# Latent scalings and rotary key-row copies: from VectorE to ScalarE in a two-layer hybrid block

## The chip, the core and the metric

The kernel runs on one core of a Trainium2 chip. A core has a matrix engine (TensorE, PE in the profile), VectorE (DVE), ScalarE (ACT), GpSimd (POOL) and SyncE (SP), whose queue here issues nearly all transfers. Each engine works through its own list of instructions in order; semaphores hold an instruction until what it needs is there. Data lies in SBUF (128 partitions) and in PSUM, where the matrix engine writes its sums. The metric is the time of one execution in microseconds. Before the change it is 857.3 us, the median of three runs (856.71 to 858.69).

## The reference, cut to what matters

Two layers, each with 512 tokens of width 1024. In each layer the normed input is projected; one part of the projection goes through an RWKV-7 recurrence, one through a gated linear recurrence, one through a latent attention with 8 heads; the three results, each gated, are projected back and added to the stream. The change lies in the latent attention:

```python
q = (rms_norm(q_lat, q_norm_g) @ w_uq).reshape(B, T, N_HEADS, QK_NOPE + QK_ROPE)
kv = (rms_norm(kv_lat, kv_norm_g) @ w_ukv).reshape(B, T, N_HEADS, QK_NOPE + V_DIM)
k_rope = apply_rope(k_rope, cos, sin)
s = jnp.einsum('bqhd,bkhd->bhqk', qn, k_nope) + jnp.einsum('bqhr,bkr->bhqk', qr, k_rope)
```

`q_lat` has 256 columns and `kv_lat` 128; each row of each is divided by its root mean square. `k_rope` has 32 columns, which all eight heads share.

## The kernel before

All tensors are fp32. A product of full precision is made of three matrix products (`mm3`, L232 to L235): each operand is split into a rounded part H, which ScalarE makes by a copy, and the rest L = x - H, which VectorE or GpSimd makes. `weights` (L217 to L230) does this for each piece of a weight matrix (tiles `wr`, `wH`, `wL`), `ysplit` (L387, through `split`, L209 to L211) for a result that goes into the output projection (tiles `c` in the profile). `copy` (L140) is a ScalarE activation that copies, with a factor if one is given.

A scheduler decides the order of the instructions on each engine from the order in the code and from its own estimates of durations, so moving an operation to another engine also shifts its neighbours. Buffers come from pools in which a new tile waits for the release of an old one: there are two rotating PSUM tiles `ps`, four PSUM accumulators `acc`, eleven SBUF tiles `g` (named `g2` in the code), three `hp` tiles.

The stage of the change comes once in each layer, in this order in the code:

- `latents(1)` (L918 to L937): for each of the four tiles `ln_t` of 128 tokens (448 columns: 256 of the query latent, 128 of the key and value latent, 32 + 32 of the rotated keys) ScalarE sums the squares (L922, L923), VectorE makes the reciprocal roots `rl` for all four tiles in one chain of small operations (L925, L926, `rsqrt` L198 to L203), and scales columns 0 to 255 (L930) and 256 to 383 (L931).
- `out_parts(1)` (L413 to L433): the output projection of the second branch, in two halves of 16 products of three; VectorE frees each accumulator at the end of a half (L428), and the second half takes the accumulators that the first leaves.
- `lat_step` (L954 to L967): PE transposes the four tiles of a column block into a `ps` tile (L962; L958 for the rotated keys), ScalarE makes H from it and VectorE L (L966).
- `ya_step` (L972 to L982): two transfers `bo` and `zz`, a product of both on GpSimd (L976), four transposes into a `ps` tile (L979), then on VectorE L980 (which also needs the GpSimd product), L981 and the split L211.
- `key_step` (L991 to L1005): for each of four pairs of heads three products and two copies of the result into `K2`; for the first pair the rotated key rows come from PSUM on ScalarE (L1001, L1002), for pairs 1 to 3 they are copied within `K2` from pair 0 (L1004, L1005), 64 partitions by 512 each.
- `value_step` and `query_step` (L1010 to L1029), then the scores, which read `K2`.

The string `Q1` (L65) mixes these steps: `a` is `ya_step`, `o` `out_parts`, `t` `lat_step`, `k`, `v` and `q` the key, value and query steps.

Of the kernel before, what the change touches and what calls it, by code (L numbers as in the profile page):

```python
# [12 lines left out]
ALU = mybir.AluOpType  # L13
# [34 lines left out]
def body(ctx, tc, x, wc, wl, wo, w2a2, gagx, wuq, wukv, vec, ln_g, fin_g, cst, out, depth=DEPTH):  # L48
    nc = tc.nc
    V, A, G = nc.vector, nc.scalar, nc.gpsimd  # L50
# [17 lines left out]
    def tl(tag, shape, dt=F32, bufs=1):  # L68
        cnt[0] += 1
        return SB.tile(list(shape), dt, tag=tag, name=f"{tag}_{cnt[0]}", bufs=bufs)  # L70

    def g2(shape=(128, 512)):
        return tl("g2", shape, F32, bufs=11)
# [10 lines left out]
    def am(shape):  # L84
        return tl("am", shape, F32, bufs=2)

    def sm(shape):
        return tl("sm", shape, F32, bufs=24)
# [21 lines left out]
    def acc(shape=(128, 512)):  # L110
        cnt[0] += 1
        return PS.tile(list(shape), F32, tag="acc", name=f"acc_{cnt[0]}", bufs=4)
# [27 lines left out]
    def copy(out, in_, **kw):  # L140
        i = A.activation(out=out, in_=in_, func=AF.Copy, **kw)  # L141
        return getattr(i, "ins", i)
# [52 lines left out]
    def rsqrt(ms, shape, tag=None):  # L195

        y, t = [tl(tag, shape, bufs=2) if tag else sm(shape) for _ in range(2)]
        V.tensor_scalar(out=y.bitcast(I32), in0=ms.bitcast(I32), scalar1=1, scalar2=None, op0=ALU.logical_shift_right)  # L198
        V.tensor_scalar(out=y.bitcast(I32), in0=y.bitcast(I32), scalar1=-1.0, scalar2=float(0x5F3759DF), op0=ALU.mult, op1=ALU.add)
        for _ in range(3):  # L200
            V.tensor_tensor(out=t, in0=y, in1=y, op=ALU.mult)
            V.scalar_tensor_tensor(out=t, in0=t, scalar=-0.5, in1=ms, op0=ALU.mult, op1=ALU.mult)
            V.scalar_tensor_tensor(out=y, in0=t, scalar=1.5, in1=y, op0=ALU.add, op1=ALU.mult)  # L203
        return y
# [12 lines left out]
    def weights(src, n=512, raw=None):  # L217

        if raw is None:
            raw = tl("wr", [128, n], F32, bufs=3)  # L220
            nc.sync.dma_start(out=raw, in_=src)
        H = tl("wH", [128, n], F32R, bufs=4)
        L = tl("wL", [128, n], F32R, bufs=4)
        wn[0] += 1
        i = copy(H, raw)
        if behind:
            tc.add_manual_dep(i, behind.pop(0).name, NOSYNC, reason="issue order")

        (V if wn[0] % wmod[0] == 0 or wn[0] <= 4 else G).tensor_tensor(out=L, in0=raw, in1=f(H), op=ALU.subtract)  # L229
        return H, L  # L230

    def mm3(o, a, b, start, stop):  # L232
        PE.matmul(o, a[0], b[0], start=start, stop=False)  # L233
        PE.matmul(o, a[0], b[1], start=False, stop=False)  # L234
        PE.matmul(o, a[1], b[0], start=False, stop=stop)  # L235
# [85 lines left out]
    def one_layer(l):  # L321
# [590 lines left out]
        def latents(part):  # L912
            if part == 0:
                for tt in range(4):
                    ln_t[tt] = g2([128, 448])
                    copy(ln_t[tt][:, 0:LAT], lat[tt])
                return
            kcos, ksin = misc["k"][:, 0], misc["k"][:, 1]  # L918
            lst = sm([128, 4, 2])
            for tt in range(4):  # L920
                j1, q = g2([128, 256]), ln_t[tt]
                A.activation(out=j1, in_=q[:, 0:256], func=AF.Square, scale=1.0 / 16.0, accum_out=lst[:, tt, 0:1])  # L922
                A.activation(out=j1[:, 0:128], in_=q[:, 256:384], func=AF.Square, scale=1.0 / 8.0, accum_out=lst[:, tt, 1:2])  # L923
            ms = sm([128, 4, 2])
            V.tensor_scalar(out=ms[:, :, 0:1], in0=lst[:, :, 0:1], scalar1=EPS, scalar2=None, op0=ALU.add)  # L925
            V.tensor_scalar(out=ms[:, :, 1:2], in0=lst[:, :, 1:2], scalar1=0.5, scalar2=EPS, op0=ALU.mult, op1=ALU.add)  # L926
            rl = rsqrt(ms, [128, 4, 2])
            for tt in range(4):
                q = ln_t[tt]
                V.tensor_scalar(out=q[:, 0:256], in0=q[:, 0:256], scalar1=rl[:, tt, 0:1], scalar2=None, op0=ALU.mult)  # L930
                V.tensor_scalar(out=q[:, 256:384], in0=q[:, 256:384], scalar1=rl[:, tt, 1:2], scalar2=None, op0=ALU.mult)  # L931
                a, b = tl("ro", [128, 32], bufs=4), tl("ro", [128, 32], bufs=4)
                V.tensor_tensor(out=a, in0=q[:, 384:416], in1=kcos[:, tt, :], op=ALU.mult)
                for d in range(2):
                    V.tensor_tensor(out=b[:, 16 * d:16 * d + 16], in0=q[:, 400 - 16 * d:416 - 16 * d], in1=ksin[:, tt, 16 * d:16 * d + 16], op=ALU.mult)
                for d in range(2):
                    V.tensor_tensor(out=q[:, 384 + 32 * d:416 + 32 * d], in0=a, in1=b, op=ALU.add)  # L937
# [4 lines left out]
        def b_split(_):  # L942
            yb[:] = [ysplit(y) for y in yb]

        steps.update({"H": chunk, "N": lambda _: group_norm(), "A": lru_a, "B": lambda i: lru_b(2 * i, 2 * i + 1), "R": b_sums, "Y": b_split,
                      "t": lat_products, "T": latents, "g": lambda p: gzc.append(gate(25 + p))})
        run(ORD2)
        run(ORD3)
# [40 lines left out]
        K2 = am([128, 4, 2, T])  # L989

        def key_step(p):  # L991
            if p == 0:
                WW["k"] = weights(wukv[l, :, 0:512])
            WK, kr = WW["k"], latT[3]
            o = acc()
            s = slice(p * 128, (p + 1) * 128)
            mm3(o, (WK[0][:, s], WK[1][:, s]), latT[2], True, True)
            copy(K2[0:64, p, 0, :], o[0:64, :])
            copy(K2[64:128, p, 1, :], o[64:128, :])
            if p == 0:  # L1000
                copy(K2[64:128, 0, 0, :], kr[0:64, :])  # L1001
                copy(K2[0:64, 0, 1, :], kr[0:64, :])  # L1002
            else:
                V.tensor_copy(out=K2[64:128, p, 0, :], in_=K2[64:128, 0, 0, :])  # L1004
                V.tensor_copy(out=K2[0:64, p, 1, :], in_=K2[0:64, 0, 1, :])  # L1005
        uvt = tl("UV", [128, 2, 2048])
        Vt = uvt[:, 0, :].rearrange("p (t h i) -> p t h i", t=4, h=8)
        PT = uvt[:, 1, :].rearrange("p (k t) -> p k t", k=4)
# [22 lines left out]
        for n, fn, c in (("k", key_step, 4), ("v", value_step, 4), ("q", query_step, 8)):  # L1031
            seqs[n] = [lambda fn=fn, i=i: fn(i) for i in range(c)]
# [193 lines left out]
```

## Time and profile before

| what | value |
| --- | --- |
| median of the runs | 857.3 us (856.71 to 858.69) |
| the profiled execution, its own time | 855.86 us |
| its span in the trace | 854.0 us |
| instructions in the trace | 15206 |
| mean granted clock of the matrix engine | 0.984 |
| stage of the change in layer 0, in layer 1 (us from the span's start) | about 298 to 325, 717 to 744 |

The profile's page gives busy times and groups of instructions by line. The trace gives more: the chain of waits (what ended last, followed back), the timeline of each engine with the idle time in front of an instruction and what ended it, and the busy time of each engine in stretches that one chooses. A group of helper lines (L141, L211, L229) is told apart by its tiles. Times in the timeline are starts and durations; a duration can overlap the next instruction's by some 0.06 us on VectorE and some 0.1 us on ScalarE, so the step from one start to the next is the better measure in a queue without gaps.

### The profile page before, as it was taken

What the parts mean: (1) busy time and instruction counts of PE and PEld (TensorE: products, weight loads), DVE (VectorE), ACT (ScalarE), POOL (GpSimd) and SP (SyncE); (2) the same over time, 40 slices, a digit from 0 to 9 for tenths busy, and PEclk for the clock granted to TensorE, in tenths of its full rate; (3) what the DMA queues carried; (4) which work ended last, traced back from release to release, by engine and by line L of the source; (5) the groups of instructions that cost most, each with busy time, mean ns of one, the idle gap of its engine ahead of it and who ended that gap; (6) DMA issues with size and microseconds to landing.
All of it is one profiled execution on the core that took longest, in us unless ns stands there. A gap on an engine that the chain in (4) does not pass through costs nothing.

```text
span 854.0 us, 15206 instructions
## 1 busy us (share of the span) xinstructions
PE 796.6 (93%) x5696; PEld 621.0 (73%) x5696; DVE 571.6 (67%) x1173; ACT 506.2 (59%) x990; POOL 325.7 (38%) x299
## 2 busy tenths in 40 slices
PE   4999999999879989999989999999998799999996
PEld 4878888877559867556778788888765697675674
DVE  5678777924886496774474966695367946877736
ACT  6667885656563536574467687846575435465644
POOL 0455557513352332012344556574143523310223
PEclk9999999999999999999999999999999899999999
DMA  7222224310123365123732233332101234731354
GB/s 245 96 74 84 72 93 136 117 51 27 32 77 97 124 197 184 51 87 99 268 124 90 75 99 101 98 111 94 29 25 41 81 107 129 241 114 50 111 173 162
DMA packets 49755, 91.08 MB, mean 107 GB/s; under 512 B 5520, under 2 KB 8336, under 8 KB 49680
## 3 DMA queue, kind: packets, MB, share of 16 engines
q1 hardware_dynamic: 49104, 89.05, 32.2%
q8 instruction: 45, 0.74, 0.4%
q10 hardware_dynamic: 576, 1.05, 0.3%
q14 instruction: 30, 0.25, 0.1%
HBM read 73.30 MB, written 16.78 MB: 105 GB/s over the span
## 4 chain that ended last, share of the span: by engine, by line
PE 69%; DVE 16%; ACT 8%; issue 3%; DMA 2%; POOL 1%; SPq 1%; ACTq 0%; DVEq 0%; POOLq 0%
PE acc L233 16%; PE acc L234 16%; PE acc L235 15%; PE acc L1058 4%; PE ck L1084 3%; ACT g L138 2%; PE ps L1076 2%; PE ps L687 1%; DVE g L681 1%; PE ps L611 1%; ACT UV L141 1%; ACT L136 1%; DVE wL L229 1%; PE ps L629 1%; PE ps L786 1%
## 5 line engine op out<-in xcount | busy, mean ns | idle before, releaser
L229 POOL TENSOR_TENSOR wL<-wr,wH 128x512 fp32r<-128x512 f32 (+1 forms) x126 | 169.7, 1350 | 290.0 <-ACT wH L141 266.0
L141 ACT ACTIVATE wH<-wr 128x512 fp32r<-128x512 f32 (+1 forms) x192 | 118.8, 622 | 140.6 <-PE acc L234 74.5
L233 PE MATMUL acc<-xH,wH 128*128 128x512 f32 (+1 forms) x496 | 192.7, 390 | 0.0
L234 PE MATMUL acc<-xL,wH 128*128 128x512 f32 (+1 forms) x496 | 189.7, 383 | 0.4 <-DVE xL L306 0.2
L235 PE MATMUL acc<-xH,wL 128*128 128x512 f32 (+1 forms) x496 | 189.1, 381 | 0.0
L233 PEld LDWEIGHTS acc<-xH,wH 128*128 128x128 f32 x496 | 94.3, 191 | 18.1 <-ACT xH L141 0.7
L235 PEld LDWEIGHTS acc<-xH,wL 128*128 128x128 f32 x496 | 94.3, 190 | 17.3
L234 PEld LDWEIGHTS acc<-xL,wH 128*128 128x128 f32 x496 | 94.4, 190 | 16.9 <-DVE xL L306 0.9
L229 DVE TENSOR_TENSOR wL<-wr,wH 128x512 fp32r<-128x512 f32 (+1 forms) x66 | 49.9, 760 | 72.8 <-ACT wH L141 72.7
L233 PE MATMUL acc<-wH,c 128*128 128x512 f32 x192 | 83.0, 432 | 2.6 <-DVE hp L428 1.3
L234 PE MATMUL acc<-wL,c 128*128 128x512 f32 x192 | 77.5, 404 | 0.5 <-DVE wL L229 0.5
L235 PE MATMUL acc<-wH,c 128*128 128x512 f32 x192 | 77.1, 402 | 0.0
L141 ACT ACTIVATE UV<-ps 64x512 f32<-64x512 f32 (+4 forms) x112 | 52.4, 494 | 30.9 <-PE ps L1076 22.6
L233 PEld LDWEIGHTS acc<-wH,c 128*128 128x128 f32 x192 | 36.7, 191 | 12.8 <-ACT c L141 3.0
L141 ACT ACTIVATE c<-g 128x512 fp32r<-128x512 f32 (+1 forms) x40 | 24.9, 630 | 34.3 <-DVE g L981 22.4
L138 ACT ACTIVATE c<-acc,sm 128x128 f32<-128x128 f32 (+3 forms) x64 | 33.6, 528 | 19.1 <-DVE sm L1060 18.8
L234 PEld LDWEIGHTS acc<-wL,c 128*128 128x128 f32 x192 | 36.9, 192 | 8.6 <-issue 1.4
L1058 PE MATMUL acc<-am,am 128*128 128x128 f32 (+3 forms) x128 | 42.3, 447 | 0.8 <-ACT c L138 0.8
L235 PEld LDWEIGHTS acc<-wH,c 128*128 128x128 f32 x192 | 36.8, 192 | 8.4 <-issue 0.5
L369 POOL TENSOR_TENSOR g<-g,g 128x512 f32<-128x512 f32 x24 | 32.1, 1338 | 24.1 <-ACT g L138 24.1
L136 ACT ACT_TABLE_LOAD x31 | 39.8, 1283 | 1.3 <-PEq L1214 0.7
L138 ACT ACTIVATE g<-g 128x512 f32<-128x512 f32 (+1 forms) x58 | 36.4, 627 | 4.6 <-DVE g L705 2.6
(222 smaller groups left out, 1592.4 us busy)
## 6 DMA issues: line engine op xcount, KB each, us to landing
wr<-in_wc_dram SPq DMA_DIRECT2D x116, 256.0 KB, 2.7
wr<-in_wo_dram SPq DMA_DIRECT2D x48, 256.0 KB, 3.4
hp<-dr SPq DMA_DIRECT2D x38, 256.0 KB, 3.2
dr<-hp SPq DMA_DIRECT2D x28, 256.0 KB, 2.1
dr<-g SPq DMA_DIRECT2D x16, 256.0 KB, 2.5
g<-dr SPq DMA_DIRECT2D x16, 256.0 KB, 3.6
wr<-in_wl_dram SPq DMA_DIRECT2D x16, 208.0 KB, 2.5
dr<-c SPq DMA_DIRECT2D x12, 256.0 KB, 3.4
```

The source lines that it names most:

```text
L136: chained(A.preload_act_table_set(SETS[st]))
L138: chained(A.activation(out=out, in_=in_, func=func, **kw))
L141: i = A.activation(out=out, in_=in_, func=AF.Copy, **kw)
L229: (V if wn[0] % wmod[0] == 0 or wn[0] <= 4 else G).tensor_tensor(out=L, in0=raw, in1=f(H), op=ALU.subtract)
L233: PE.matmul(o, a[0], b[0], start=start, stop=False)
L234: PE.matmul(o, a[0], b[1], start=False, stop=False)
L235: PE.matmul(o, a[1], b[0], start=False, stop=stop)
L369: G.tensor_tensor(out=z, in0=z, in1=s, op=ALU.mult)
L611: PE.matmul(os[e][:, cp, :].rearrange("p (x s) -> p x s", x=2), bk[rr, ch, :, :].rearrange("p x s -> p (x s)"), ar[rr, :, ch * 64:(ch + 1) ...
L1058: PE.matmul(o[:, 0:n], qT[:, hd, qt * 128:n], K2[:, p, e, 0:n], start=True, stop=True)
L1076: PE.transpose(o[:, (qt - kt) * 128:(qt - kt + 1) * 128], Pm[p][e, qt][:, kt * 128:(kt + 1) * 128], ident)
L1084: i = PE.matmul(ot[e * 64:(e + 1) * 64, k2 * 128:T], Vt[:, k2, 2 * p + e, :], PT[:, 2 * (k2 % 2) + e, 0:(4 - k2) * 128], start=(k2 == 0), ...
```

## The change

Eight scalings in each layer (L930, L931, four tiles) and six copies in each layer (L1004, L1005, three pairs) are issued on ScalarE, as activations that copy, the scalings with the column of `rl` as factor. Their operands, results and places in the code are the same.

```diff
@@ latents @@
-                V.tensor_scalar(out=q[:, 0:256], in0=q[:, 0:256], scalar1=rl[:, tt, 0:1], scalar2=None, op0=ALU.mult)
-                V.tensor_scalar(out=q[:, 256:384], in0=q[:, 256:384], scalar1=rl[:, tt, 1:2], scalar2=None, op0=ALU.mult)
+                copy(q[:, 0:256], q[:, 0:256], scale=rl[:, tt, 0:1])
+                copy(q[:, 256:384], q[:, 256:384], scale=rl[:, tt, 1:2])
@@ key_step @@
-                V.tensor_copy(out=K2[64:128, p, 0, :], in_=K2[64:128, 0, 0, :])
-                V.tensor_copy(out=K2[0:64, p, 1, :], in_=K2[0:64, 0, 1, :])
+                copy(K2[64:128, p, 0, :], K2[64:128, 0, 0, :])
+                copy(K2[0:64, p, 1, :], K2[0:64, 0, 1, :])
```

The scheduler's order shifts with it, in both layers alike. On ScalarE in layer 0 the scalings come behind the split of a weight (`wH_3342`); the last two of them and what follows read now (`g_509` is the fourth latent tile, `c_558` the first `ysplit`, `wH_3360` and `wH_3378` weights of the second half of `out_parts`, `c_584` to `c_588` the latents of `lat_step`):

```order
L141 ACTIVATE g_509_2938<-g_509_2938,sm_3071 128x256
L141 ACTIVATE g_509_2938<-g_509_2938,sm_3071 128x128
L141 ACTIVATE c_558_3137<-g_556_3126 128x512
L141 ACTIVATE wH_3360<-wr_3358 128x512
L141 ACTIVATE wH_3378<-wr_3376 128x512
L141 ACTIVATE c_584_3241<-ps_3236,vecs 128x512
L141 ACTIVATE c_586_3249<-ps_3244,vecs 128x512
```

`wH_3360` stood in front of `c_558` before and now stands behind it and behind all eight scalings.

On VectorE in layer 0, in the second half of the stage, from the third latent on (`c_588` the third latent, the tiles `g_591`, `g_595` and `g_599` are the `zz` of `ya_step` 1, 2 and 3, `am_3122` is `K2`), the order was before:

```order
L966 SCALAR_TENSOR_TENSOR c_588_3257<-ps_3252,vecs,c_588_3257 128x512
L1004 COPY am_3122<-am_3122 64x512 x3
L980 SCALAR_TENSOR_TENSOR g_591_3266<-ps_3270,vecs,g_591_3266 128x512
L1005 COPY am_3122<-am_3122 64x512
L981 TENSOR_TENSOR g_591_3266<-g_591_3266,g_590_3265 128x512
L980 SCALAR_TENSOR_TENSOR g_595_3281<-ps_3285,vecs,g_595_3281 128x512
```

and in the changed kernel:

```order
L966 SCALAR_TENSOR_TENSOR c_588_3257<-ps_3252,vecs,c_588_3257 128x512
L980 SCALAR_TENSOR_TENSOR g_591_3266<-ps_3270,vecs,g_591_3266 128x512
L981 TENSOR_TENSOR g_591_3266<-g_591_3266,g_590_3265 128x512
L980 SCALAR_TENSOR_TENSOR g_595_3281<-ps_3285,vecs,g_595_3281 128x512
L211 TENSOR_TENSOR c_593_3277<-g_591_3266,c_593_3277 128x512
L981 TENSOR_TENSOR g_595_3281<-g_595_3281,g_594_3280 128x512
```

The copies are gone from between L966 and the `ya_step` chain. On ScalarE, at the same place, they now stand in two groups of three ahead of the splits of that chain (`c_593`, `c_597`):

```order
L141 ACTIVATE am_3122<-ps_3260 64x512 x2
L141 ACTIVATE wH_3408<-wr_3406 128x512
L141 ACTIVATE am_3122<-am_3122 64x512 x3
L141 ACTIVATE c_593_3277<-g_591_3266 128x512
L141 ACTIVATE am_3122<-am_3122 64x512 x3
L141 ACTIVATE c_597_3292<-g_595_3281 128x512
```

On PE the transposes of the third latent block move from the last accumulator of a weight's round to the third, and three products of the key step move behind a value step. On SP a load (`bo` of `ya_step` 2) moves ahead of one store, and two weight loads of the query step move ahead of four stores of L430. GpSimd's order is the same.

## The prediction

> **What bounds the kernel now.** The page comes first: busy times, and the chain of work that ended last.
>
> ```profile
> PE 796.6 (93%) x5696; PEld 621.0 (73%) x5696; DVE 571.6 (67%) x1173; ACT 506.2 (59%) x990; POOL 325.7 (38%) x299
> PE 69%; DVE 16%; ACT 8%; issue 3%; DMA 2%; POOL 1%; SPq 1%; ACTq 0%; DVEq 0%; POOLq 0%
> ```
>
> The kernel as a whole belongs to PE, but 16% of the chain is VectorE's, and that share is an average over stages. So the stage of the change is cut out, by the busy times of a stretch (columns: PE, PEld, DVE, ACT, POOL, granted clock, share and rate of the transfers). The first two rows are the stage in layer 0 and in layer 1, the last two a finer cut in layer 0.
>
> ```profile
> 298.40:323.90 25.50, 22.26 (x98) 16.33 (x96) 24.82 (x41) 9.89 (x18) 8.09 (x6) 0.93 0.58 194
> 717.60:743.05 25.45, 22.23 (x98) 16.17 (x96) 25.09 (x41) 9.88 (x18) 8.06 (x6) 0.93 0.57 194
> 300.00:304.00 4.00, 2.14 (x12) 1.29 (x10) 4.00 (x11) 0.68 (x2) 0.16 (x1) 1.00 0.05 12
> 304.00:308.00 4.00, 3.91 (x10) 3.09 (x11) 4.00 (x7) 1.62 (x3) 1.03 (x1) 0.57 0.91 292
> ```
>
> VectorE is busy for 24.82 of 25.50 us here, ScalarE for 9.89: in this stage VectorE is the limit and ScalarE has room, in both layers alike. PE sits idle for almost half of 300 to 304, and then its granted clock drops to 0.57. The chain of waits over this stretch (start, us, what) says the same in order:
>
> ```profile
> 298.42 0.07 DVE g L930
> ...
> 301.42 0.66 DVE g L980
> 302.08 0.60 DVE wL L229
> 302.68 0.60 DVE g L981
> 303.28 0.67 DVE hp L428
> ...
> 305.23 0.43 PE acc L235
> ...
> 308.21 0.44 PE ps L962 x4
> ...
> 310.61 1.77 DVE am L1004 x2
> ...
> 323.29 0.61 DVE wL L229
> 323.90 0.04 issue
> 324.44 0.23 PE ps L235
> ```
>
> VectorE from the scalings to L428, which frees the first accumulator; a stretch of PE; then VectorE again from the key copies to a weight's rest at 323.90, when PE goes on. All edited lines lie on this chain.
>
> **What the change takes off VectorE.** Its timeline, with the GpSimd instructions that run beside it:
>
> ```profile
> 298.69 0.28 DVE L931 TENSOR_SCALAR g<-g,sm 128x128 f32<-128x128 f32 x1
> 298.89 1.42 DVE L930 TENSOR_SCALAR g<-g,sm 128x256 f32<-128x256 f32 x1
> 301.15 0.27 DVE L931 TENSOR_SCALAR g<-g,sm 128x128 f32<-128x128 f32 x1
> 310.18 2.19 DVE L1004 COPY am<-am 64x512 f32<-64x512 f32 x3
> 312.41 0.75 DVE L980 SCALAR_TENSOR_TENSOR g<-ps,vecs,g 128x512 f32<-128x512 f32 x1
> 313.08 1.29 DVE L1005 COPY am<-am 64x512 f32<-64x512 f32 x1
> 314.29 0.67 DVE L981 TENSOR_TENSOR g<-g,g 128x512 f32<-128x512 f32 x1
> 315.56 1.09 DVE L1005 COPY am<-am 64x512 f32<-64x512 f32 x1
> 318.44 0.41 DVE L1005 COPY am<-am 64x512 f32<-64x512 f32 x1
> 298.86 1.30 POOL L229 TENSOR_TENSOR wL<-wr,wH 128x512 fp32r<-128x512 f32 x1 [0.50 <-POOL g L976]
> 312.81 1.28 POOL L976 TENSOR_TENSOR g<-g,g 128x512 f32<-128x512 f32 x1 [0.72 <-DMA g<-dr]
> 315.08 1.29 POOL L976 TENSOR_TENSOR g<-g,g 128x512 f32<-128x512 f32 x1 [0.99 <-PE acc L235]
> ```
>
> The eight scalings last from 298.42 in the chain to 301.42: 3.0 us. The six copies: 310.18 to 312.41 is 2.2, 313.08 to 314.29 is 1.2, 315.56 to the next instruction about 1.0, the last 0.3: 4.7 us. Together 7.7 us of VectorE in each layer. A lone copy takes 0.41; those that run beside a GpSimd instruction take 1.29 and 1.09, the scaling 1.42. Without these collisions the edits would weigh 4 x 0.47 + 6 x 0.35 = 4.0 us (the chain's step from 298.42 to 298.69 and the next to 298.89 for a tile; a copy's 0.41 less the overlap).
>
> On this the Trainium skill, SBUF — State Buffer, "Who interferes with whom", says that VectorE's copies and scalings in their two-port mode and GpSimd take a shared port for a whole instruction, and whoever comes second is blocked. The rows agree (the copy at 313.08 ends 0.3 after GpSimd's 312.81 + 1.28). By the page ScalarE is outside this, and all 7.7 us go; were it blocked in the same way, three operations in a layer would last about 1 us longer there, which would just use up the room that step 5 finds.
>
> **What it adds on ScalarE.** These operations in these forms are not in the trace; the nearest groups are:
>
> ```profile
> L922 ACT ACTIVATE g<-g 128x256 f32<-128x256 f32 x8 | 3.2, 406 | 0.0
> L923 ACT ACTIVATE g<-g 128x128 f32<-128x128 f32 x8 | 2.3, 294 | 0.0
> L141 ACT ACTIVATE g<-g,sm 128x512 f32<-128x512 f32 x4 | 2.9, 718 | 1.4 <-DVE sm L256 1.4
> L141 ACT ACTIVATE wH<-wr 128x512 fp32r<-128x512 f32 x176 | 110.0, 628 | 125.7 <-PE acc L234 72.2 <-issue 13.7 <-DMA wr<-in_wo_dram 12.7
> L141 ACT ACTIVATE am<-ps 64x512 f32<-64x512 f32 x4 | 2.3, 583 | 0.1
> ```
>
> A factor from a column costs 0.09 (718 against 628). A scaling of 256 columns then takes 0.40 to 0.50, one of 128 columns 0.29 to 0.38; back to back some 0.1 overlaps. I take 0.40 + 0.29 per tile: 2.8 us for eight (1.9 to 3.5). A copy takes 0.58 to 0.63, 0.5 in a row: 3.2 us for six (up to 3.8). ScalarE's 9.9 us in the stage become 16 of some 21: it stays below VectorE and PE, but it is strictly in order, so what counts is where these stand.
>
> **The new order, walked through layer 0.** VectorE steps by 0.60, and by 0.66 with a PSUM operand (301.42, 302.08, 302.68, 303.28). Products step by 0.23, four transposes by 0.44, as the chain shows. The other rows that the walk needs:
>
> ```profile
> 304.09 0.71 PE L233 MATMUL acc<-wH,c 128*128 128x512 f32 x1 [1.30 <-DVE hp L428]
> 324.97 0.40 PE L233 MATMUL acc<-c,wH 128*128 128x512 f32 x1
> 309.02 0.32 SPq L975 DMA_DIRECT2D g<-dr  x1
> 310.13 0.41 SPq L975 DMA_DIRECT2D g<-dr  x1
> ```
>
> 1. VectorE is free at 298.40 and goes L229, L980, L981, L428: the first accumulator is free at 300.9 instead of 303.95. ScalarE scales from 298.4 to 301.2; the fourth tile's first part is there at 301.0, so PE, which comes to the transposes at 300.6, waits 0.4 at most. It starts the second half of `out_parts` at 301.65 instead of 304.09.
> 2. Here the order costs something: `c_558` stands behind the scalings on ScalarE (done 301.8), L211 waits for it on VectorE, and the three L428 and two L966 queue behind: L211 to 302.45, L428 to 304.45, L966 to 305.8. PE waits 0.8 for the second accumulator and 1.05 for the PSUM tile that L966 frees (305.15). `wH_3360` comes at 302.4, long before PE needs it.
> 3. Are these gaps enough to lower the clock again? Before, PE stood for 0.53 and 1.30 us within 3 us, with only eight transposes between. Now there are products in between; I take no drop. One drop costs some 8 products at 0.43 instead of 0.23, 1.6 us.
> 4. PE is through the third block of transposes and the first weight at 309.05 and has 34 products left: done at 316.85.
> 5. `ya_step` 2 waits for its transfer: its `zz` goes out at 309.02 before, and GpSimd starts at 312.81, 3.8 later; that of `ya_step` 3 goes out at 310.13 and GpSimd starts at 315.08. Their buffers come free with the L958 transposes, now done at 306.25; so GpSimd runs for `ya_step` 2 from 309.9 to 311.2, and for 3 until 313.3. VectorE takes L980 at 311.2, L211, then L981 (which collides with GpSimd, until 313.9), L980, L981, L211, L229, L211 and the first L428 from 316.95 to 317.6. ScalarE's two groups of copies are done by 311.6, `c_597` at 312.2; VectorE needs it at 315.1.
> 6. The first accumulator of the second half is then free at 317.6; PE, done at 316.85, waits 0.8, and does 15 products to 321.1. Before, the same 15 were behind PE at 324.97.
>
> Gain: 324.97 - 321.1 = 3.9 us. From there to 338 PE runs without a gap and the order is the old one; the swapped loads and stores on SP, and PE's three moved products, lie under these 13 us and cost nothing, but up to 0.7 if PE had to wait for them. Layer 1 has the same rows shifted by 419.1 us, so 7.8 us in all: 855.86 of the profiled execution (1.86 outside its span) becomes 848.1. The median of the runs lies 1.44 above it, so 849.5.
>
> **Bounds.** Above: 63 products and 28 transposes from 300.6 take 17.6 us, to 318.2; that is 6.8 us a layer, 13.5 in all, 843.8. Below: the dearest scalings (+0.7, all on the path) and one drop of the clock (+1.6) leave 1.6 us a layer, 854.1; the slowest copies (+0.6) stay within the 2.9 us of step 5.
>
> **Rivals.** The change that weighs less (a): the chain moves to the transfers of `ya_step`. The transfer engines are 91% busy from 304 to 308 above; if the `zz` of `ya_step` 2 lands 1.7 us later than I take it, the gain is 2.2 a layer: 852.9. For it speaks that GpSimd's wait at 312.81 is for that transfer; against it that the transfers ahead of it go out some 3 us sooner too. The change that weighs more (b): if `zz` lands early and L211 doesn't wait, PE's own work is the limit but for about 1.3 us: 5.5 a layer, 846.3. No change (c): PE's freed time is given back at the scores, as VectorE has a chain there; against it speaks that the scores wait for the query products, which all come earlier. 857.3.
>
> Slower (d): ScalarE takes VectorE's place on the chain. Without collisions the pieces cost 4.0 on VectorE and 6.0 on ScalarE; if they lie on the path in full, that is 2 us a layer more, 861.3. It decides from where `c_597`, behind both groups of copies, comes later than VectorE's need: 2.9 us over six copies, so from about 1.0 us a copy instead of 0.5. Against it stands the highest row above, 0.63. The Trainium skill, ScalarE: Activation LUTs, "Rules for kernel authors", speaks for (d): multiplications belong on VectorE, not on ScalarE. By that rule the sum is 861.3; the trace agrees with it for a lone operation (0.41 against 0.58), not for a stage where VectorE is 97% busy.
>
> **How the numbers follow.** Forecast 0.62 (847.0 to 852.0), (a) 0.17, (b) 0.12, (c) 0.05, (d) 0.04. A measurement of this kernel can tell about 0.2% from no change, 855.6 to 859.0. So faster 0.91, same 0.05, slower 0.04. The range leaves out (c), (d), half of (b) and a part of (a): 845.5 to 853.5.
>
> **What would show it.** Right: VectorE under 18.5 us busy in the stage and no collision longer than 1.4; the scalings within 3 us on ScalarE, PE's wait for the first L428 gone (the row with 1.30), the granted clock of that stretch at 1.00, and the GpSimd product of `ya_step` 2 done about 13 us after the last L203 (15.7 before). Wrong: PE waits for ScalarE rows of `am` or `c`; that product starts over 13.5 us after the last L203; or a second stretch with a clock near 0.5 behind the scalings.

## The result and the profile after

| | before | after |
| --- | --- | --- |
| median of the runs, us | 857.64 (856.71 to 858.69) | 852.2 (850.58 to 854.13) |
| profiled execution, its own time | 855.86 | 854.13 |
| its span in the trace | 854.0 | 852.3 |
| mean granted clock of TensorE | 0.984 | 0.986 |

The ratio is 0.9937, with a 95% interval of 0.9912 to 0.9962: 5.4 us less. (The table has a fourth run of before; ahead of the prediction there were three, with a median of 857.3.) The two profiled executions lie only 1.7 us apart, since that of before is faster than all four runs of the table and that of after is the slowest of its four; in it the stage of the change also begins 2.0 us later, for reasons outside the stage. So stages are compared here, each from its own first instruction.

The busy times and the chain of waits on the page of the kernel after:

```profile
PE 793.0 (93%) x5696; PEld 619.7 (73%) x5696; DVE 561.1 (66%) x1145; ACT 518.6 (61%) x1018; POOL 326.3 (38%) x299
...
PE 65%; DVE 15%; ACT 10%; DMA 4%; issue 3%; POOL 3%; SPq 0%; ACTq 0%; DVEq 0%; POOLq 0%
```

VectorE lost 10.5 us and ScalarE gained 12.4; what is new is DMA and GpSimd (POOL) on the chain, 4% and 3% instead of 2% and 1%. The stage by the busy times of stretches (PE, PEld, DVE, ACT, POOL, granted clock, share and rate of the transfers), layer 0 and layer 1, and the four microseconds in which the clock had dropped to 0.57:

```profile
300.40:323.95 23.55, 21.08 (x102) 16.10 (x101) 19.35 (x28) 17.50 (x33) 8.32 (x6) 1.00 0.69 217
715.90:741.50 25.60, 21.98 (x108) 17.03 (x106) 19.59 (x28) 17.50 (x33) 10.10 (x7) 1.00 0.64 207
...
304.00:308.00 4.00, 2.49 (x12) 1.45 (x11) 4.00 (x7) 2.07 (x5) 2.53 (x2) 1.00 0.82 265
```

VectorE was busy 24.8 us in the stage and is now at 19.4; the granted clock stays at 1.00. TensorE's timeline in layer 0, those rows in which it waits, with the first transpose of the stage and the first score product behind it:

```profile
302.64 1.25 PE L962 MATMUL ps<-C,g 128*128 128x128 f32 x8
...
305.33 0.50 PE L233 MATMUL acc<-wH,c 128*128 128x512 f32 x1 [0.74 <-DVE hp L428]
...
307.30 0.66 PE L962 MATMUL ps<-C,g 128*128 128x128 f32 x4 [0.78 <-DVE c L966]
...
320.45 0.47 PE L233 MATMUL acc<-c,wH 128*128 128x512 f32 x1 [0.96 <-DVE hp L428]
...
336.88 1.65 PE L1058 MATMUL acc<-am,am 128*128 128x128 f32 x8
```

From the first transpose to the first score product: 34.24 us. The same two rows of the kernel before:

```profile
300.62 0.99 PE L962 MATMUL ps<-C,g 128*128 128x128 f32 x4
...
337.94 1.64 PE L1058 MATMUL acc<-am,am 128*128 128x128 f32 x8
```

That is 37.32, so layer 0 gains 3.08 us. Layer 1 gains 2.08 (35.16 against 37.24): there the last of TensorE's waits is longer:

```profile
737.98 0.47 PE L233 MATMUL acc<-c,wH 128*128 128x512 f32 x1 [2.50 <-DVE hp L428]
```

The two stages together give 5.2 us, about the difference of the medians; outside them the profiled execution of after is 3.5 us longer than that of before, which is why the two executions differ by 1.7 only. I call this length **the stage** below: two rows of TensorE, the same for every kernel. What ends last inside it, by the chain of waits over layer 0 (start, us, what):

```profile
300.49 2.01 ACT g L141 x6
...
303.37 0.53 ACT c L141
303.92 0.69 DVE c L211
...
309.92 0.53 ACT wH L141
310.51 1.28 POOL wL L229
311.81 0.09 issue
311.90 1.61 POOL g L976
313.54 0.75 DVE g L980
...
319.56 0.75 DVE hp L428
```

The reader sees the scalings, now on ScalarE, then `c` behind them, and in the second half GpSimd: a weight's rest, the product of `ya_step` 2, and only then VectorE. The copies are not on it.

### The profile page after: what moved, and what is told of

Its sections match the earlier page's. It is cut to its first block, busy times and chain, and to the rows that moved or that the text cites. A ratio compares the mean times of both kernels' runs of the same rounds, so it can differ in the third digit from the quotient of the medians.

```text
span 852.3 us, 15212 instructions
## 1 busy us (share of the span) xinstructions
PE 793.0 (93%) x5696; PEld 619.7 (73%) x5696; DVE 561.1 (66%) x1145; ACT 518.6 (61%) x1018; POOL 326.3 (38%) x299
## 3 DMA queue, kind: packets, MB, share of 16 engines
q10 hardware_dynamic: 576, 1.05, 0.3%
## 4 chain that ended last, share of the span: by engine, by line
PE 65%; DVE 15%; ACT 10%; DMA 4%; issue 3%; POOL 3%; SPq 0%; ACTq 0%; DVEq 0%; POOLq 0%
PE acc L233 15%; PE acc L234 14%; PE acc L235 14%; PE acc L1058 4%; PE ck L1084 3%; ACT g L138 3%; PE ps L1076 2%; ACT wH L141 1%; ACT UV L141 1%; PE ps L687 1%; DMA hp<-dr 1%; DVE g L681 1%; PE ps L611 1%; ACT L136 1%; PE ps L629 1%
## 5 line engine op out<-in xcount | busy, mean ns | idle before, releaser
L229 POOL TENSOR_TENSOR wL<-wr,wH 128x512 fp32r<-128x512 f32 (+1 forms) x126 | 170.4, 1355 | 298.2 <-ACT wH L141 270.7
L234 PEld LDWEIGHTS acc<-xL,wH 128*128 128x128 f32 x496 | 94.5, 190 | 16.9 <-DVE xL L306 0.9
L229 DVE TENSOR_TENSOR wL<-wr,wH 128x512 fp32r<-128x512 f32 (+1 forms) x66 | 50.9, 774 | 72.2 <-ACT wH L141 72.2
L233 PE MATMUL acc<-wH,c 128*128 128x512 f32 x192 | 81.9, 427 | 1.4 <-DVE hp L428 1.1
L235 PE MATMUL acc<-wH,c 128*128 128x512 f32 x192 | 76.1, 397 | 0.0
```

## The experiments

Three things are turned on and off: the scalings and the copies (the two halves of the change), and the loads of `ya_step` 2 and 3. Four more kernels are told of in the text behind the table. Medians are given with the ratio to the kernel before, timed beside them; stages in us, layer 0 / layer 1.

| run | scalings on | copies on | loads early | median, us | ratio (95%) | stage |
| --- | --- | --- | --- | --- | --- | --- |
| before | DVE | DVE | no | 858.6, 858.1, 858.4 | 1 | 37.3 / 37.2 |
| e_copy | DVE | ACT | no | 858.34 | 0.9999 (0.9984 to 1.0014) | 37.2 / 38.8 |
| e_scal | ACT | DVE | no | 852.03 | 0.9927 (0.9909 to 0.9945) | 35.1 / 35.1 |
| after_re | ACT | ACT | no | 853.66 | 0.9947 (0.9932 to 0.9963) | 34.4 / 34.2 |
| b_q | DVE | DVE | yes | 855.30 | 0.9964 (0.9952 to 0.9976) | 36.0 / 35.9 |
| c_q | DVE | ACT | yes | 854.23 | 0.9948 (0.9931 to 0.9965) | 35.0 / 34.9 |
| a_q | ACT | ACT | yes | 850.36 | 0.9909 (0.9892 to 0.9926) | 33.0 / 33.0 |
| s_q | ACT | DVE | yes | 849.57 | 0.9897 (0.9877 to 0.9918) | 32.8 / 32.8 |
| s_v | ACT | DVE | yes, and a split later | 846.93 | 0.9873 (0.9857 to 0.9890) | 32.3 / 32.3 |

**Each half alone.** `e_scal` is the change without the hunk in `key_step`, `e_copy` without the hunk in `latents`:

```diff
 e_scal = after, with
-                copy(K2[64:128, p, 0, :], K2[64:128, 0, 0, :])
+                V.tensor_copy(out=K2[64:128, p, 0, :], in_=K2[64:128, 0, 0, :])
...
 e_copy = after, with
-                copy(q[:, 0:256], q[:, 0:256], scale=rl[:, tt, 0:1])
+                V.tensor_scalar(out=q[:, 0:256], in0=q[:, 0:256], scalar1=rl[:, tt, 0:1], scalar2=None, op0=ALU.mult)
...
```

> The scalings alone go to ScalarE; the six key copies stay on VectorE. Theory T (VectorE's 3.0 us of scalings lie on the path in full, c behind them on ScalarE gives 0.8 back, and from then on the copies with their collisions hold VectorE as before): PE starts the second half of out_parts about 2.4 us earlier, and some 2.0 to 2.2 us a layer are left behind the last weight's rest: 853.2 to 853.6. Rival S (a gain goes by VectorE time taken away, without a common limit: 3.0 of 7.7): 2.1 of the 5.4 us, 855.5. Rival: the scalings carry nothing (the time lost before the first L428 is given back at the copies): 857.6.

> The copies alone go to ScalarE; the scalings stay on VectorE, so everything up to the first L428 stands as before (PE waits 1.3 us there and the granted clock drops again in layer 0). Theory T (behind the copies the chain goes over ya_step's transfers and GpSimd's products, which start no earlier than before, about 312.8 and 315.1): VectorE takes L981 at about 314.2 and L980 at 316.4, the first L428 of the second half ends some 1.3 us earlier than before: 1.2 to 1.5 us a layer, 854.6 to 855.2. The parts then add up to more than the whole (4.2 and 2.7 against 5.4). Rival S (by VectorE time taken away, 4.7 of 7.7): 3.3 us, 854.3, and the parts add up to the whole.

The scalings alone bring 0.9927, as much as the whole change; the copies alone nothing, 0.9999. Of `e_scal` the first theory is the nearer one: the stage gains 2.2 and 2.1 as it said, the time lies 1.2 below its range. So the ratio gives 6.3 us where the two stages give 4.3; the other 2.0 are not in the stages of the profiled execution. Of `e_copy` both numbers were wrong. The waits on TensorE's timeline in layer 0 of `e_scal` (0.74, 0.78 and the row of the first view below) add up to 3.2 us, those of before (1.30 and the rows of the second view) to 3.1:

```profile
319.90 0.47 PE L233 MATMUL acc<-c,wH 128*128 128x512 f32 x1 [1.66 <-DVE hp L428]
```

```profile
302.14 0.66 PE L962 MATMUL ps<-C,g 128*128 128x128 f32 x4 [0.53 <-DVE g L980]
...
313.22 0.66 PE L979 MATMUL ps<-C,c 128*128 128x128 f32 x4 [0.93 <-DVE g L980]
...
320.76 0.50 PE L233 MATMUL acc<-c,wH 128*128 128x512 f32 x1 [0.30 <-DVE hp L428]
```

TensorE waits as long as before, but no longer runs at half clock for 3.4 us in between: in `e_scal` its granted clock is 1.00 from 300 to 338.

In layer 1 the stage of `e_copy` is 1.5 us longer than before; there the clock is at 0.50 a second time, from 743.25 to 746.66. VectorE's timeline in `e_copy`, layer 0, shows where the freed time went:

```profile
312.46 0.75 DVE L980 SCALAR_TENSOR_TENSOR g<-ps,vecs,g 128x512 f32<-128x512 f32 x1 [0.81 <-PE ps L979]
...
315.56 0.75 DVE L980 SCALAR_TENSOR_TENSOR g<-ps,vecs,g 128x512 f32<-128x512 f32 x1 [1.50 <-PE acc L235]
...
318.70 0.75 DVE L980 SCALAR_TENSOR_TENSOR g<-ps,vecs,g 128x512 f32<-128x512 f32 x1 [1.19 <-POOL g L976]
...
321.95 2.06 DVE L428 SCALAR_TENSOR_TENSOR hp<-acc,sm,hp 128x512 f32<-128x512 f32 x3
```

Where copies stood, VectorE now waits 3.5 us ahead of three L980, and the first L428 begins 19.9 us after the first transpose (302.09), no sooner than before (319.97 - 300.62 = 19.4). GpSimd's timeline of the same run shows what they wait for: the product of `ya_step` 2 comes late, behind a weight's rest and a wait of 0.71, and that of `ya_step` 3 waits for its load:

```profile
312.22 1.29 POOL L229 TENSOR_TENSOR wL<-wr,wH 128x512 fp32r<-128x512 f32 x1 [2.59 <-ACT wH L141]
314.22 1.30 POOL L976 TENSOR_TENSOR g<-g,g 128x512 f32<-128x512 f32 x1 [0.71 <-DVE g L981]
317.00 1.67 POOL L976 TENSOR_TENSOR g<-g,g 128x512 f32<-128x512 f32 x1 [1.47 <-DMA g<-dr]
```

The load for the row at 314.22 went out at 310.52, 3.7 us earlier; in before it is 3.8 from the same issue to the product (309.02 to 312.81, and there the row names the transfer). What is named at 314.22 is L981, so the row alone doesn't settle it. But the copies were time that VectorE would otherwise have waited.

**The loads.** The query tile `qT` is empty until the query steps, so `ya_step` 2 and 3 can load into its slices; these four loads no longer wait for the latents' buffers and go out before the stage.

```diff
         ya = []
+        K2 = am([128, 4, 2, T])
+        qT = am([128, 8, T])
         def ya_step(p):
-            bo, zz = g2(), g2()
+            bo, zz = (g2(), g2()) if p < 2 else (qT[:, 2 * p, :], qT[:, 2 * p + 1, :])
...
-        K2 = am([128, 4, 2, T])
...
-        qT = am([128, 8, T])
```

> The kernel after, with the two tensors of ya_step 2 and 3 (bonus and gate) loaded into slices of the query tile, which is empty until the query steps, instead of two buffers each of the pool g: their four loads no longer wait for the latents' transposes and go out before the stage. Theory T (what is left of the gain forecast is held by these loads and by GpSimd behind them): VectorE's waits for GpSimd's product (1.19 and 2.57 us) go, PE's wait for the first L428 of the second half (0.96 in layer 0, 2.50 in layer 1) shrinks to under 0.8 in both, and the time falls by 2.0 to 3.5 us against the kernel after: 848.7 to 850.2. Rival V (VectorE's own queue is the next limit, the loads lie beside it): PE's waits stay as they are, at most 0.7 us: 851.5 to 852.2.

> The kernel before, with the same two steps' loads into slices of the query tile and nothing else. Theory T (before the change VectorE is the limit of the stage and the transfers lie beside its work; they become the limit only once the copies are off it): at most 0.5 us a layer, 856.6 to 857.6, and VectorE still over 23 us busy in the stage. Rival L (the loads were already the limit before): as much as in the kernel after, 2.0 to 3.5 us, 854.1 to 855.6.

In `a_q` (this edit on after) TensorE no longer waits for the first L428 of the second half in either layer; the stage falls to 33.0 in both, the time to 850.36. The theory holds in its mechanism; the time lies 0.2 above its range (848.7 to 850.2). What is left of waits in layer 0:

```profile
304.88 0.50 PE L233 MATMUL acc<-wH,c 128*128 128x512 f32 x1 [0.74 <-DVE hp L428]
...
306.85 0.66 PE L962 MATMUL ps<-C,g 128*128 128x128 f32 x4 [0.78 <-DVE c L966]
```

In `b_q` (the edit on before) the price was wrong: it brings 3.1 us, not at most 1.0. The mark of the theory held (VectorE is busy for 23.6 and 23.8 us in the stage), so VectorE was still busy nearly throughout, and hardly waited for loads. But the loads were not something beside its work: with GpSimd's products out of the stage the copies collide less (before, two of them took 1.29 and 1.09 beside such a product), and two of the six could be placed behind L428.

**The two halves again, without the loads.**

> Scalings on ScalarE, loads of ya_step 2 and 3 into the query tile (as in a_q), key copies on VectorE (as in before). It asks whether the copies are worth anything once the loads no longer hold VectorE. Theory T (the copies were hidden behind the loads' wait; without that wait they take VectorE's time on the path): five copies stand ahead of the first L428 of the second half, about 1.9 us and 1.0 of collisions, of which some 1.4 fall into VectorE's idle time and 1.0 into PE's slack (PE comes 1.0 after L428 in a_q): 0.6 to 0.9 us a layer more than a_q, 851.5 to 852.2 beside a_q's 850.4. Rival C (the copies are worth nothing anywhere): 850.4, as a_q.

> Copies on ScalarE, loads moved as in a_q, scalings on VectorE (as in before). Theory T: the first half of the stage stays as before (waits of 0.53 and 1.30, the clock's drop); behind it PE's wait of 0.92 for L980's successor behind the copies goes, and nothing else, since PE is slow there: 0.9 us a layer less than b_q, 853.5 beside b_q's 855.3. From s_q and this the stage's length from the first transpose to the first score product should be about 35.1 (b_q 36.0, a_q 33.0). Rival C (the copies are worth nothing anywhere): 855.3.

With the scalings on ScalarE the copies' place still makes no difference: `s_q` (copies on VectorE) has 32.8, `a_q` 33.0. The rival was right, and for both engines: that the copies gave nothing isn't due to the loads alone. In `s_q` the copies fill VectorE's gaps, and the first L428 ends at 318.6, some 0.7 us before TensorE comes to it (1.1 in `a_q`); in `a_q` the copies stand ahead of `c` on ScalarE, and VectorE waits 0.62 for that. Only with the scalings on VectorE and the loads early do the copies weigh something: `c_q` has 35.0 against `b_q`'s 36.0, as the theory had it (its wait of 0.92 goes); in time 0.5 to 0.7 us a layer, but there the two intervals overlap.

`c_q` against `a_q` shows what the scalings alone are worth when the loads and the copies are out of the way: 2.0 us a layer of the stage. TensorE's waits in `c_q` are nearly as long as in `a_q` (0.53 and 1.30 against 0.74 and 0.78: 0.3 us more), but between them stand only four short transposes, where `a_q` has products, and the clock drops behind them. Busy times of `c_q` in stretches, layer 0:

```profile
303.65:307.06 3.41, 1.59 (x8) 1.08 (x9) 3.41 (x7) 1.39 (x3) 0.00 (x0) 1.00 0.31 83
307.06:310.47 3.41, 3.41 (x10) 2.55 (x9) 3.41 (x6) 0.92 (x2) 1.28 (x1) 0.50 0.93 293
```

Half the clock for 3.41 us is 1.7 us of products, and 0.3 + 1.7 makes the 2.0. That holds only if VectorE would have come along: in `c_q` the first L428 of the second half ends 0.75 us before TensorE comes to it, less than the 1.7.

**Is it the clock?** An attempt to keep TensorE busy through these waits with useless transposes, on `c_q` and on before:

```diff
-            for tt in range(4):
+            for tt in [0, 1, 2, 3] * (2, 4, 1)[s]:
                 PE.transpose(p[:, tt * 128:(tt + 1) * 128], ln_t[tt][:, s * 128:(s + 1) * 128], ident)
```

> c_q with useless work for TensorE: the first group of the latents' transposes is done twice and the second four times (the same data into the same place), 16 transposes a layer, which fill the waits of 0.53 and 1.30 us; nothing else is changed. Theory K (where the loads no longer hold the stage, c_q's 35.0 us against a_q's 33.0 are the granted clock: TensorE's waits ahead of the second half of out_parts lower it to 0.5 for 3.4 us, and with the scalings on ScalarE these waits fall apart and it stays at 1.00): the granted clock stays at 1.00, the stage falls to 33.3 to 33.8, the time by 2.4 to 3.4 us, to about 851. Rival W (the waits themselves are the loss, and the clock's drop lies beside other work): stage and time as in c_q, 35.0 and 854.2, or longer.

> The kernel before with the same useless transposes. If the granted clock stays at 1.00 here too, this tells what the clock alone was worth in the kernel before. Theory T (before the change VectorE's chain sets the end of the stage, whatever TensorE's clock does in between): TensorE reaches the first L428 of the second half 1.7 us earlier and waits there instead (0.30 becomes about 1.7): stage 36.9 to 37.5, at most 0.4 us a layer, 857.2 to 858.1. Rival K2 (the drop is the loss here too): 1.7 us a layer, 854.7.

Both got slower, 859.76 (ratio 1.0018, 1.0009 to 1.0028) and 862.84 (1.0059, 1.0040 to 1.0078), with stages of 37.7 and 39.3. The 24 transposes do fill the two waits; but the scheduler's order changes with them: it moves the third group of transposes ahead of nine of the products, and there TensorE waits for a PSUM tile, 2.7 us at a stretch:

```profile
302.53 3.48 PE L962 MATMUL ps<-C,g 128*128 128x128 f32 x24
306.00 0.47 PE L233 MATMUL acc<-wH,c 128*128 128x512 f32 x1
309.14 0.81 PE L962 MATMUL ps<-C,g 128*128 128x128 f32 x4 [2.68 <-DVE c L966]
309.60 0.78 PE L234 MATMUL acc<-wL,c 128*128 128x512 f32 x1
```

The clock then drops again, from 309.5 to 312.9. So these two runs moved the hole and did not answer the question.

The other runs can say more, since each has its mean granted clock, not the profiled ones alone. An estimate: one minus this clock, times the run's span, is the time lost to half clock wherever TensorE is the limit. Means over the runs of a kernel, in us, with the standard errors (how far such a mean may be off by chance) of the last two in brackets:

| kernel | runs | time | lost to the clock | the rest |
| --- | --- | --- | --- | --- |
| before (beside `e_scal`) | 23 | 858.4 | 15.3 (0.3) | 843.1 (0.3) |
| e_scal | 6 | 851.9 | 11.2 (0.2) | 840.8 (0.4) |
| e_copy | 12 | 858.1 | 16.1 (0.5) | 842.0 (0.3) |
| after, after_re | 4, 6 | 852.3, 853.4 | 12.1 (0.4), 12.5 (0.5) | 840.2 (0.9), 840.9 (0.1) |
| c_q | 11 | 854.1 | 16.4 (0.7) | 837.7 (0.5) |
| a_q | 5 | 850.4 | 13.1 (0.6) | 837.3 (0.7) |

`c_q` and `a_q` differ by 3.4 us in the clock and by 0.4 in the rest, which is inside the errors (the kernel before, timed beside each, has 15.7 and 15.3): the reading of the rows above holds over all their runs. Of the 6.5 us between before and `e_scal` 4.1 are the clock, and of the whole change's 5 to 6 us about 3. It stays an estimate, since these means are of whole executions, with every drop outside the stage in them.

**What is left of the price.** In after and `a_q`, the split of `ya_step` 0 (`c` on ScalarE) comes behind the scalings, and L211 waits for it on VectorE with three L428 and two L966 behind. `v1q` is `a_q` with that split written behind the block of `out_parts`; `a_q8` is `a_q` with the loads of all four steps early, so that step 0 is done before the stage. The edit of `v1q`:

```diff
-            ya.append(ysplit(zz))
+            if p == 0:
+                ya.append(zz)
+            else:
+                if p == 1:
+                    ya[0] = ysplit(ya[0])
+                ya.append(ysplit(zz))
```

> a_q with the split of ya_step 0 (c on ScalarE, L211 on VectorE) written behind the block of out_parts instead of ahead of it: the three L428 and two L966 no longer stand behind a wait for c, which comes behind the scalings on ScalarE. Theory T (this wait is what is left of the scalings' price: PE waits 0.74 and 0.78 us a layer): both waits go, 1.2 to 1.5 us a layer, 847.3 to 848.0. Rival R (the time is lost again at the first L428 of the second half, since VectorE's queue there is full): under 0.4 us a layer, 849.6 to 850.4.

> a_q with the loads of all four steps in the query tile: ya_step 0 then has its data long before the stage, its two VectorE operations and its split go ahead of the group norm's end, and four buffers of g come free. Theory T: the waits of 0.74 and 0.78 us go here too, by another way, and VectorE has 2 us less in the stage: 1.2 to 1.5 us a layer less than a_q, 847.3 to 848.0. Rival R: VectorE's operations that moved ahead delay the scalings by their 1.3 us, and the gain is lost there: 850.4.

`v1q`: 849.44 (0.9895, 0.9869 to 0.9920), stage 32.4 in both layers: 0.6 shorter than `a_q`, half of what was expected. The wait of 0.74 is gone; that for L966 is 1.07 instead of 0.78, since a weight's L229 now stands ahead of it. `a_q8` has the shortest stage of all, 31.8 in both layers, yet a median of 852.96 (0.9938, 0.9914 to 0.9961) from runs between 849.38 and 856.8. Its profile is of the fastest run, so it doesn't show what the others lose. In that profile the clock is at 0.50 from 423.4 to 433.7, outside the stage, where `a_q` has 431.7 to 435.1, and from the first score product of layer 0 to the first transpose of layer 1 it takes 385.4 us, where `a_q` has 383.0 and before 381.9. So in this execution a part of the stage's gain is lost again between the stages; that the earlier stage is the reason is possible, and not shown. Neither kernel reached the 847.3 to 848.0 of its theory.

**The change again, and the best of the parts.**

> The kernel after itself, unchanged, timed beside the three below. Theory T (the scalings carry the whole gain, the copies nothing): the same ratio as the scalings alone had, 0.9927 (0.9909 to 0.9945), so 851.3 to 852.3. Rival: the copies carry something beside the scalings: a ratio under 0.990.

> Three edits together: the scalings on ScalarE, the loads of ya_step 2 and 3 in the query tile, the split of ya_step 0 behind the block of out_parts; the key copies stay on VectorE. Theory T (the copies lie in PE's slack once the loads do not hold VectorE): the stage from the first transpose to the first score product is 32.2 to 32.4 us, as in v1q (32.4) with the copies on ScalarE; 848 to 849.5, the fastest or level with v1q. Rival (with the first half 0.6 shorter the copies come out of the slack): 33 us or more, 850.5.

`after_re`, 0.9947, agrees with the first measurement (0.9937); its time, 853.66, lies above the 851.3 to 852.3 of its theory and further still from its rival. Its stages, 34.4 and 34.2, are 0.7 and 0.9 shorter than those of `e_scal`, while its time isn't shorter: whether the copies bring or cost a microsecond within the whole change, these intervals can't say. `s_v` (the edits of `a_q` and `v1q`, the copies back on VectorE) is the fastest kernel of the study, 846.93, 11.5 us below before and 6.7 below the change timed beside it; its stage is 32.3, as expected, its time 1.1 below the range. Beside `v1q` (849.44, the copies on ScalarE) the intervals overlap. Its one wait in layer 0, and VectorE at the second half:

```profile
304.89 0.66 PE L962 MATMUL ps<-C,g 128*128 128x128 f32 x4 [1.07 <-DVE c L966]
```

```profile
314.05 0.41 DVE L1011 COPY am<-am 64x512 f32<-64x512 f32 x1
...
315.07 0.42 DVE L1010 COPY am<-am 64x512 f32<-64x512 f32 x1
315.53 2.07 DVE L428 SCALAR_TENSOR_TENSOR hp<-acc,sm,hp 128x512 f32<-128x512 f32 x3
...
318.78 0.41 DVE L1011 COPY am<-am 64x512 f32<-64x512 f32 x1
```

The copies are back at 0.41 each: with GpSimd's products out of the way nothing collides with them.

## The prediction, step by step

The time was forecast at 849.5 in a range of 845.5 to 853.5; it is 852.2. Faster was right, the gain was put too high: 3.9 us a layer against 3.1 and 2.1 in the first profile, 2.9 and 3.1 in the second (`after_re`).

**What comes off VectorE** (7.7 us a layer): VectorE's busy time in the stage falls by 5.5 only, to 19.4 where under 18.5 was to show it right, mostly since other collisions (up to 1.64, where 1.4 was the mark) took the place of those that went. And it says little as a weight: the forecast has no split of its gain between the two parts, and by themselves they are worth 6.3 us by the ratio or 4.3 by the stages (scalings) and nothing (copies).

**ScalarE's prices.** Rows of the kernel after, layer 0:

```profile
300.49 2.88 ACT L141 ACTIVATE g<-g,sm 128x256 f32<-128x256 f32 x8 [2.07 <-DVE sm L203]
...
310.46 1.92 ACT L141 ACTIVATE am<-am 64x512 f32<-64x512 f32 x3
```

2.88 for eight scalings (2.8 forecast), 0.64 a copy in a row (0.5 forecast, 0.63 the bound). These copies ran beside GpSimd's row at 310.51 and were not stretched (in `a_q` a copy with no GpSimd instruction beside it takes 0.63), as the Trainium skill, SBUF — State Buffer, "Who interferes with whom", has it for ScalarE.

**Steps 1 to 3** held. The second half of `out_parts` starts 1.01 us after the first transpose (1.05 forecast). `c` behind the scalings costs TensorE 0.74 and 0.78 (0.8 and 1.05). The clock doesn't drop. In layer 1 TensorE's wait of 2.50 could have brought a drop; that it didn't is luck of its place (see the last section).

**Steps 4 to 6: here the size is off.** TensorE is through with the half 16.85 after the first transpose instead of 16.25; step 4 leaves out four transposes of a `ya_step` (0.4). The product of `ya_step` 2 ends at 10.9 in layer 0 (10.6 forecast; 13.0 after the last L203, as the mark had it), but for another reason than the one given: the walk had it wait for its transfer and didn't see the weight's rest at 310.51 ahead of it on GpSimd. In layer 1 it ends at 11.6, and begins 13.6 after the last L203, just past the mark for wrong (13.5). There the transfer seems to be late: the load goes out at 724.35, 5.25 before the product (3.6 in layer 0, 3.8 before the change), the three transfers of that moment take 5.1 us or more to land, and the weight's rest has ended at 727.81:

```profile
726.52 1.29 POOL L229 TENSOR_TENSOR wL<-wr,wH 128x512 fp32r<-128x512 f32 x1 [3.17 <-ACT wH L141]
729.60 1.29 POOL L976 TENSOR_TENSOR g<-g,g 128x512 f32<-128x512 f32 x1 [1.79 <-issue]
```

In layer 0 VectorE then meets GpSimd twice, not once:

```profile
311.06 1.29 DVE L981 TENSOR_TENSOR g<-g,g 128x512 f32<-128x512 f32 x1
...
314.21 1.64 DVE L211 TENSOR_TENSOR c<-g,c 128x512 fp32r<-128x512 f32 x1
```

The first L428 begins at 16.9 in layer 0 instead of 16.35, and the wait of 0.8 in step 6 becomes 0.96 and 2.50 (1.29 and 1.02 in the second profile). This is rival (a), the loads and what queues behind them: in part in layer 0, in full in layer 1 of the first profile, where the gain is 2.1 and rival (a) had 2.2. Its 852.9 is nearer to the result than the forecast. `a_q` confirms the mechanism: with the loads out, this wait is nil and the stage 1.2 to 2.2 shorter.

**The other rivals.** (b), 846.3, needed an early load and an L211 that doesn't wait: `s_v` has both, at 846.9, the change has neither. (c) and (d) fell. For (d) the Trainium skill, ScalarE: Activation LUTs, "Rules for kernel authors", had spoken: keep multiplications on VectorE. For the scalings the runs speak against it (6.3 us gained), since VectorE was late there and ScalarE stood idle for 2.07 us ahead of them; for the copies, which are worth nothing on ScalarE, they speak for leaving them. Whether copies as dear as 1.0 us would have made (d) true wasn't tried.

## What to carry to other kernels

Time taken off the busiest engine counts only where another engine waits for what it does next and it isn't about to wait itself: look at the next waits in both lists (here a product on GpSimd behind a late load, and, with the loads early, TensorE, which in `s_q` came 0.7 us after VectorE) before adding up durations, and time the halves of a change apart. Where a load waits for a buffer, a tile that is allocated but not yet written is one for free. A price in engine time is not a price on the path: 3.0 us of VectorE in each layer, in front of two waits of TensorE that lay close together, gave 6.3 us in time over both layers, a good part of it by the clock, and 4.7 us in each layer behind them gave nothing.

## What the hardware showed beside this

The granted clock of TensorE fell to 0.50 for 3.4 us behind stretches of 3.41 us in which TensorE was busy for 1.46 (before, 300.75 to 304.16), 1.59 (`c_q`) and 0.73 us (`c_qf`). In `a_q` the waits of 0.74 and 0.78 leave 1.9 us in the emptiest stretch of that length (303.60 to 307.01), and the clock stays at 1.00. The busy times of that stretch of before, and of that of `a_q` (columns as above):

```profile
300.75:304.16 3.41, 1.46 (x10) 0.81 (x8) 3.41 (x9) 0.84 (x2) 0.00 (x0) 1.00 0.09 25
```

```profile
303.60:307.01 3.41, 1.90 (x8) 0.94 (x7) 3.41 (x6) 2.02 (x4) 2.52 (x2) 1.00 0.53 178
```

The Trainium skill, TensorE: Matmul & The Clock Gate, "What's actually happening", has the half clock follow an idle window of about 3.4 us; the length agrees, but TensorE was 43% busy in the window of before.

How empty a stretch is doesn't decide alone. In layer 1 of after, TensorE's wait of 2.50 leaves 0.91 us in the first stretch below, and the clock stays at 1.00:

```profile
734.57:737.98 3.41, 0.91 (x6) 0.44 (x4) 3.38 (x7) 2.26 (x5) 1.35 (x1) 1.00 0.07 12
733.11:736.52 3.41, 2.37 (x11) 1.63 (x9) 3.38 (x6) 2.27 (x5) 0.32 (x1) 1.00 0.08 29
736.52:739.93 3.41, 1.95 (x9) 1.64 (x10) 3.41 (x7) 1.52 (x4) 1.67 (x1) 1.00 0.46 106
```

The drops in before begin at 252.95, 304.15, 433.85, 672.79 and 723.99, which are 15, 38, 70 and 15 steps of 3.413 us apart, and those of every other run lie on such a raster too, each on its own. The raster of after (drops at 432.74 and 671.67) cuts the wait of 2.50 in two, and the last two rows are its stretches: 2.37 and 1.95 us busy. Along the rasters of all fourteen traces, from 60 to 840 us, every stretch with under 1.47 us of TensorE was followed by half clock, and none with over 1.80 was, if it ran at full clock itself; between the two both occur. So whether a wait costs 1.7 us more hangs on where it falls on the raster, which a change elsewhere in the program can shift.

Drops also lie elsewhere in the program, at other places from kernel to kernel, and runs of one kernel differ by up to 7 us (`a_q8`); a stage in the trace is mostly the steadier measure (37.3 and 37.2 in before, 33.0 and 33.0 in `a_q`, but 37.2 and 38.8 in `e_copy`).

GpSimd also stretches VectorE's smallest operations: of the chain of 128x8 that makes the reciprocal roots, each instruction takes 0.17, and one beside a GpSimd product (298.20, 1.29 long) 1.28 (`e_copy`):

```profile
298.03 0.17 DVE L203 SCALAR_TENSOR_TENSOR sm<-sm,sm 128x8 f32<-128x8 f32 x1
298.23 1.28 DVE L201 TENSOR_TENSOR sm<-sm 128x8 f32<-128x8 f32 x1
```
